# Hybrid decoder layer on one core: a weight chunk split ahead of the query/key rotations, and the last norm's 1/sqrt by ScalarE's estimate and one Newton step

## The chip, the cores and the metric

One core of one Trainium2 chip runs the whole layer in one launch. The metric is the device time of an execution in microseconds (us); three executions of the kernel before gave 813.43, 814.51 and 815.0 us, so its median is 814.51 us. The engines are called as the profile calls them: PE (TensorE matmul), PEld (its weight load), DVE (VectorE), ACT (ScalarE), POOL (GpSimd), SP (the queue that issues most DMAs).

## What is computed

One layer on 512 tokens of width 1024, all in float32. It has three sub-layers, each with a norm before and after: attention and retention in parallel, cross-attention to 256 memory rows, and a SwiGLU feed-forward.

```python
def rms_norm(x, g):
    y = x * lax.rsqrt(jnp.mean(x * x, axis=-1, keepdims=True) + 1e-6)
    return y * g

def hybrid_mixer(h, w_in, attn_gn_g, ret_gn_g, w_out):
    proj = h @ w_in                                  # 1024 -> 3*512 + 4*512
    aq, ak, av, rq, rk, rv, rg = jnp.split(proj, splits, axis=-1)
    a = dilated_attention(rope(aq), rope(ak), av)    # 8 heads x 64, then a norm per head
    r = retention(rope(rq), rope(rk) * 128 ** -0.5, rv)   # 4 heads x 128, then a group norm
    r = jax.nn.silu(rg) * r
    return jnp.concatenate([a, r], axis=-1) @ w_out

def reference(x, mem, ...):
    x = x + rms_norm(hybrid_mixer(rms_norm(x, pre_mix_g), ...), post_mix_g)
    x = x + rms_norm(memory_cross_attn(rms_norm(x, pre_mem_g), mem, ...), post_mem_g)
    x = x + rms_norm(swiglu(rms_norm(x, pre_ffn_g), w_gate_up, w_down), post_ffn_g)
    return x
```

## The kernel before, in words

**Split weights.** Each float32 operand of a projection is kept as a high part and a low part, and each product takes three matmuls: high by high, high by low, low by high (`mm3`, L84 to L86). A weight chunk of 128 x 2048 floats (1 MB) arrives by a DMA from SP into one of two `raw` buffers (L152). `split` then makes the high part `wh` on ACT (L90, two pieces of 128 x 1024) and the low part `wl` on DVE (L91, two pieces); `wl` needs `wh`. Each pair `wh`, `wl` takes two of the 20 buffers ("units") of one pool, which also holds the transposed input, the rotation tables, and the queries and keys. `take` hands a chunk over and splits further ones in advance; `ahead` splits up to a named chunk. Chunks of `w_in` are numbered as they are used: 0 to 3 retention's queries and keys, 4 and 5 its values, 6 and 7 its gate, 8 and up attention.

**The place of the first edit.** The first stage makes retention's queries and keys, in eight tiles f = 0 to 7 that fill all eight PSUM banks (`rqk`, `pss`). After the first half of the sum the kernel calls `ahead("w_in", 4)`, computes the input's row norm, and finishes the eight tiles one after the other. The norm factor is spread to all partitions by four small matmuls (`bcast_row`, L222) and multiplied into the rotation tables on POOL (L288). Then each tile is rotated: three DVE instructions (L291 to L293, into `t1` and `t2`) and an addition on POOL (L294). Tile 0 is first copied to `sc`, so its rotation reads SBUF alone; the others read PSUM. A bank is free again once its rotation has read it. Then `tok_proj(4, "rv", ...)` makes the values: four token blocks, each 24 matmuls, 12 with chunk 4 and 12 with chunk 5. After them come the gate's blocks (`rg`, chunks 6 and 7).

**What sets the order.** Outside of the feed-forward, which is written out by hand, a scheduler orders the instructions of each engine at build time, by the order of the code, the free buffers and its own costs. On the chip every engine works its list strictly in that order and waits on semaphores. So DVE's list decides when a low part is made, and a rotation that stands ahead of it must be done first. SP's list is ordered likewise: a `raw` buffer is filled again once both parts of the chunk in it are made.

**The place of the second edit.** The feed-forward's last product is made for four blocks of 128 rows, each in two halves of 512 columns (tile `dn`). `residual` (L664 to L676) closes a block: for each half ACT squares it with a row sum (L670), DVE multiplies it by the gain (L671, tile `z`) and adds the sum to `v` (L672, tile `pv`); then `rsqrt` (L180 to L184) makes 1/sqrt(v) on DVE from an integer guess and three Newton steps of two instructions; then `z` times this factor is added to `x` (L676), and two DMAs write the block out, one from SP's queue, one from ACT's (L1065). Nothing stands behind the last block, so its `residual` is the kernel's end.

Of the kernel before, what the change touches and what calls it, by code (L numbers as in the profile page):

```python
# [15 lines left out]
AF = mybir.ActivationFunctionType  # L16
ALU = mybir.AluOpType
AX = mybir.AxisListType

P = 128  # L20
D = 1024
# [3 lines left out]
TB = S // P  # L25
# [6 lines left out]
EPS = 1e-6  # L32
# [6 lines left out]
def hybrid_layer(ctx, tc, t, out):  # L39
    nc = tc.nc  # L40
# [9 lines left out]
    def uname(p):  # L50
        cnt[0] += 1
        return f"{p}{cnt[0]}"

    def bank(name):
        return psp.tile([P, 512], F32, tag="ps", name=uname(name))
# [10 lines left out]
    def row(name):  # L66
        return wk.tile([P, D], F32, tag="w4k", name=uname(name), bufs=2)

    def junk():
        return wk.tile([P, D], BF16, tag="junk", name=uname("junk"), bufs=1)  # L70

    def small(shape, name):
        big = math.prod(shape[1:]) > 8
        return sm.tile(shape, F32, tag="big" if big else "tiny", name=uname(name), bufs=2 if big else 32)
# [67 lines left out]
    def load(pieces=1, swap=False):  # L142
        key = chunks.pop(0)
        src = t[key[0]][key[1]]
        raw = fetched.pop(key, None)
        w = pair("w")
        if raw is None:
            raw = rawp.tile([P, 2048], F32, tag="raw", name=uname("raw"))
            n = 2048 // pieces
            for i in range(pieces):  # L150
                c = slice(i * n, (i + 1) * n)
                nc.sync.dma_start(raw[:, c], src[:, c])  # L152
        n = 2048 // max(2, pieces)
        for i in range(max(2, pieces)):
            c = slice(i * n, (i + 1) * n)
            if swap and i == 0:
                nc.vector.tensor_copy(w[0][:, c], raw[:, c])
                nc.vector.tensor_sub(w[1][:, c], raw[:, c], w[0][:, c].bitcast(F32))
            else:
                split(raw[:, c], w[0][:, c], w[1][:, c])  # L160
        loaded[key] = w

    def take(name, i, ahead=2):
        while (name, i) not in loaded:
            load()
        while chunks and len(loaded) - 1 < ahead:
            load()
        return loaded.pop((name, i))

    def ahead(name, i):  # L170
        while (name, i) in chunks:
            load()

    def rsqrt(v, n, name, e=None):
        e = e or nc.vector
        y = small([P, n], name + "y")
        w = small([P, n], name + "w")
        if n == 1:
            nv = small([P, 1], name + "n")
            e.tensor_scalar(y.bitcast(I32), v.bitcast(I32), -0.5, 1597463007.0, op0=ALU.mult, op1=ALU.add)  # L180
            e.tensor_scalar_mul(nv, v, -0.5)
            for _ in range(3):
                e.tensor_scalar(w, y, y, nv, op0=ALU.mult, op1=ALU.mult)
                e.tensor_scalar(y, w, 1.5, y, op0=ALU.add, op1=ALU.mult)  # L184
            return y
        nc.vector.tensor_scalar(y.bitcast(I32), v.bitcast(I32), -0.5, 1597463007.0, op0=ALU.mult, op1=ALU.add)
        for _ in range(3):
            nc.vector.tensor_mul(w, y, y)
            nc.vector.scalar_tensor_tensor(w, w, -0.5, v, op0=ALU.mult, op1=ALU.mult)
            nc.vector.scalar_tensor_tensor(y, w, 1.5, y, op0=ALU.add, op1=ALU.mult)  # L190
        return y

    def row_rstd(rows, n, width, name, eps=EPS, e=None):
        ss = small([P, n], name + "s")
        for i, r in enumerate(rows):
            nc.scalar.activation(junk()[:, :width], r, AF.Square, accum_out=ss[:, i:i + 1])
        v = small([P, n], name + "v")
        (e or nc.vector).tensor_scalar(v, ss, 1.0 / width, eps, op0=ALU.mult, op1=ALU.add)
        return rsqrt(v, n, name, e)
# [8 lines left out]
    def load_gains(*names):  # L208
        u = unit("g")
        out = []  # L210
        for i, name in enumerate(names):
            src = t[name]
            out.append(u[:, i * D:(i + 1) * D])
            nc.sync.dma_start(out[-1], bass.AP(tensor=src.tensor, offset=src.offset, ap=[[0, P], [1, D]]))
        return out
# [25 lines left out]
    ones = cp.tile([P, P], F32, name="ones")  # L241
# [13 lines left out]
    w_rqk = [take("w_in", i, 0) for i in range(4)]  # L255
# [8 lines left out]
    pss = [bank("rqk") for _ in range(8)]  # L264

    def rqk(f, k):
        w = w_rqk[k // 2]
        mm3(pss[f], part(w, (k % 2) * D + f * P, P), hx(k, 0, S), k == 0, k == KT - 1)

    for k in range(4):  # L270
        for f in range(8):
            rqk(f, k)
    ahead("w_in", 4)
    rstd0 = row_rstd(x, TB, D, "r0")
    rbc = None
    for f in range(8):
# [191 lines left out]
    scale = AD ** -0.5  # L468
# [190 lines left out]
    att_out(3)  # L659
    w_out = {c: take("w_out", c, 0) for c in (2, 3, 0, 1)}  # L660

    def residual(pss, b, g, e=None, cuts=((0, 512), (512, 512))):
        e = e or nc.vector
        ss = small([P, len(cuts)], "ps")  # L664
        z = row("z")
        v = small([P, 1], "pv")
        for i, (c0, n) in enumerate(cuts):
            c = slice(c0, c0 + n)
            ps = pss[c0 // 512][:, c0 % 512:c0 % 512 + n]
            nc.scalar.activation(junk()[:, :n], ps, AF.Square, accum_out=ss[:, i:i + 1])  # L670
            nc.vector.tensor_mul(z[:, c], ps, g[:, c])  # L671
            e.tensor_scalar(v, ss[:, i:i + 1], 1.0 / D, v if i else EPS, op0=ALU.mult, op1=ALU.add)  # L672
        rs = rsqrt(v, 1, "pr", e)
        for c0, n in cuts:
            c = slice(c0, c0 + n)
            nc.vector.scalar_tensor_tensor(x[b][:, c], z[:, c], rs, x[b][:, c], op0=ALU.mult, op1=ALU.add)  # L676
# [44 lines left out]
    def mix_half(hf, mid=None):  # L721
        bs = (2 * hf, 2 * hf + 1)
        pss = out_proj(bs, y_lhs, w_out, order, "o1", 2, mid)
        hs = []
        for b in bs:
            e = nc.gpsimd if b == 3 else nc.vector
            residual(pss[b], b, g1, e)
            hs.append(normed(b, g2, e))
        return hs
# [102 lines left out]
    def mem_block(b, mid=None):  # L832
        pss = out_proj((b,), o_lhs, wo, nat, "o2", 0, mid)[b]
        with tc.high_priority(600):
            residual(pss, b, g3, nc.vector)
            return normed(b, g4, nc.vector)
# [195 lines left out]
    pss = [[bank("dn") for _ in range(2)] for _ in range(TB)]  # L1032
# [3 lines left out]
    cuts = [halves] * TB  # L1036

    def down(b, c0, n, k, w):
        mm3(pss[b][c0 // 512][:, c0 % 512:c0 % 512 + n], part(aT[k // 4], (k % 4) * S + b * P, P),
            part(w, (k % 2) * D + c0, n), k == 0, k == FT - 1)  # L1040

    for c in range(FT // 2 - NL):
        if c % 2 == 0:
            split_a(c // 2 + 1)
        w = take("w_dn", c)
# [8 lines left out]
    g5, = load_gains("post_ffn_g")  # L1054
# [4 lines left out]
    for b in range(TB):  # L1059
        for c0, n in cuts[b]:  # L1060
            for k in range(FT - 2 * NL, FT):
                down(b, c0, n, k, ws[k // 2 - (FT // 2 - NL)])
        residual(pss[b], b, g5, cuts=cuts[b])
        for i, (c0, n) in enumerate(cuts[b]):
            (nc.sync, nc.scalar)[i % 2].dma_start(out[b * P:(b + 1) * P, c0:c0 + n], x[b][:, c0:c0 + n])  # L1065

# [95 lines left out]
```

## Time and profile before

| | |
|---|---|
| median of the three runs | 814.51 us (813.43 to 815.0) |
| the profiled execution's own time | 813.49 us |
| its span, first to last instruction | 811.7 us |
| busy: PE, DVE, ACT, POOL | 97%, 62%, 47%, 24% of the span |
| mean granted TensorE clock | 0.994 |

In a row of the timeline stand the start in us, the duration in us, engine, line, operation, output and input, and the count where equal rows were merged; in brackets stands the idle time of the engine before it and what ended this idle time. The chain of waits lists who waited for whom: total us, times, longest. Matmuls overlap: each takes 0.39 us in the rows, but at full clock one starts every 0.227 us.

### The profile page before, as it was taken

What the parts mean: (1) busy time and instruction counts of PE and PEld (TensorE: products, weight loads), DVE (VectorE), ACT (ScalarE), POOL (GpSimd) and SP (SyncE); (2) the same over time, 40 slices, a digit from 0 to 9 for tenths busy, and PEclk for the clock granted to TensorE, in tenths of its full rate; (3) what the DMA queues carried; (4) which work ended last, traced back from release to release, by engine and by line L of the source; (5) the groups of instructions that cost most, each with busy time, mean ns of one, the idle gap of its engine ahead of it and who ended that gap; (6) DMA issues with size and microseconds to landing.
All of it is one profiled execution on the core that took longest, in us unless ns stands there. A gap on an engine that the chain in (4) does not pass through costs nothing.

```text
span 811.7 us, 12194 instructions
## 1 busy us (share of the span) xinstructions
PE 790.5 (97%) x4828; PEld 696.5 (86%) x4828; DVE 503.5 (62%) x1007; ACT 384.4 (47%) x664; POOL 196.8 (24%) x169
## 2 busy tenths in 40 slices
PE   9989999999999999999999989999999999999995
PEld 8767888876777888999988989999999998888884
DVE  6496158865565646857656697667777766541144
ACT  6504343557555642535527386555555545432011
POOL 0161024330110110210000463333333326551000
PEclk9999999999999999999999999999999999999998
DMA  8616211231112650414205468777777783764011
GB/s 328 255 52 233 105 52 53 94 114 53 53 52 104 258 209 1 156 54 160 100 27 141 145 164 251 209 208 207 209 208 209 210 258 132 308 245 169 1 52 52
DMA packets 23849, 119.55 MB, mean 147 GB/s; under 512 B 2800, under 2 KB 2800, under 8 KB 14320
## 3 DMA queue, kind: packets, MB, share of 16 engines
q1 hardware_dynamic: 19904, 99.89, 33.3%
q0 software_dynamic: 3168, 17.83, 12.0%
q10 hardware_dynamic: 720, 1.06, 0.3%
q8 instruction: 38, 0.62, 0.3%
q14 instruction: 19, 0.16, 0.1%
HBM read 108.80 MB, written 9.96 MB: 146 GB/s over the span
## 4 chain that ended last, share of the span: by engine, by line
PE 76%; DVE 12%; issue 4%; POOL 3%; ACT 3%; DMA 1%; DVEq 0%; SPq 0%; ACTq 0%; POOLq 0%
PE dn L84 5%; PE dn L86 5%; PE dn L85 5%; PE p L84 3%; PE o L85 3%; PE p L86 3%; PE p L85 3%; PE o L84 3%; PE o L86 3%; PE q L85 3%; PE q L86 3%; PE q L84 3%; DVE wl L91 3%; PE r L84 2%; PE r L85 2%
## 5 line engine op out<-in xcount | busy, mean ns | idle before, releaser
L91 DVE TENSOR_TENSOR wl<-raw,wh 128x1024 fp32r<-128x1024 f32 (+1 forms) x91 | 118.0, 1330 | 66.1 <-ACT wh L90 39.6
L90 ACT CAST wh<-raw 128x1024 fp32r<-128x1024 f32 (+1 forms) x91 | 90.1, 1038 | 69.4 <-DMA raw<-in_w_in 37.9
L91 DVE TENSOR_TENSOR wbl<-sums,wbh 128x1024 fp32r<-128x1024 f32 x40 | 51.2, 1280 | 30.3 <-ACT wbh L90 30.3
L84 PE MATMUL dn<-wh,ah 128*128 128x512 f32 x176 | 68.5, 389 | 0.0
L85 PE MATMUL dn<-wl,ah 128*128 128x512 f32 x176 | 68.5, 389 | 0.0
L86 PE MATMUL dn<-wh,al 128*128 128x512 f32 x176 | 68.5, 389 | 0.0
L135 POOL DMA_DIRECT2D wal<-in_w_gu x22 | 19.6, 889 | 176.3 <-ACT wal L134 117.7
L1022 POOL TENSOR_TENSOR al<-af,ah 128x512 fp32r<-128x512 f32 x22 | 36.1, 1672 | 43.9 <-ACT ah L1021 43.9
L84 PE MATMUL p<-bB,wah 128*128 128x256 f32 x160 | 45.3, 283 | 0.0
L85 PE MATMUL p<-bB,wah 128*128 128x256 f32 x160 | 45.3, 283 | 0.0
L86 PE MATMUL p<-bB,wal 128*128 128x256 f32 x160 | 45.3, 283 | 0.0
L90 ACT CAST wbh<-sums 128x1024 fp32r<-128x1024 f32 x40 | 40.2, 1051 | 3.3 <-POOL sums L125 1.8
L125 POOL TENSOR_TENSOR sums<-raw,sums 128x512 f32<-128x512 f32 x20 | 34.1, 1704 | 25.4 <-DVE sums L125 25.4
L86 PEld LDWEIGHTS dn<-wh,al 128*128 128x128 f32 x176 | 33.0, 188 | 6.9
L85 PEld LDWEIGHTS dn<-wl,ah 128*128 128x128 f32 x176 | 33.0, 188 | 6.8
L84 PEld LDWEIGHTS dn<-wh,ah 128*128 128x128 f32 x176 | 33.0, 188 | 6.8
L134 ACT ACTIVATE wal<-wah 128x768 fp32r<-128x768 f32 (+1 forms) x48 | 36.6, 810 | 0.0
L85 PE MATMUL q<-hhl,wh 128*128 128x256 f32 x128 | 36.2, 284 | 0.2 <-DVE hhl L91 0.2
L84 PE MATMUL q<-hhh,wh 128*128 128x256 f32 x128 | 35.8, 284 | 0.3 <-ACT hhh L90 0.3
L86 PE MATMUL q<-hhh,wl 128*128 128x256 f32 x128 | 36.1, 283 | 0.0
L131 ACT CAST wah<-raw 128x768 fp32r<-128x768 f32 (+1 forms) x48 | 35.9, 804 | 0.0
L915 ACT ACTIVATE c<-c 128x512 f32<-128x512 f32 x20 | 12.6, 632 | 49.1 <-DVE c L914 49.1
(337 smaller groups left out, 2522.2 us busy)
## 6 DMA issues: line engine op xcount, KB each, us to landing
raw<-in_w_gu SPq DMA_DIRECT2D x22, 1024.0 KB, 5.0
wal<-in_w_gu POOLq DMA_DIRECT2D x20, 768.0 KB, 7.5
raw<-in_w_in SPq DMA_DIRECT2D x12, 1024.0 KB, 4.9
raw<-in_w_dn SPq DMA_DIRECT2D x11, 1024.0 KB, 4.8
raw<-in_w_kv SPq DMA_DIRECT2D x8, 1024.0 KB, 4.7
ad<-c SPq DMA_DIRECT2D x20, 256.0 KB, 4.1
af<-ad SPq DMA_DIRECT2D x5, 1024.0 KB, 7.0
x<-in_x SPq DMA_DIRECT2D x4, 1024.0 KB, 9.7
```

What stands on the lines that cost most here:

```text
L84: nc.tensor.matmul(o, lhsT=sh, rhs=mh, start=start, stop=False)
L85: nc.tensor.matmul(o, lhsT=sh, rhs=ml, start=False, stop=False)
L86: nc.tensor.matmul(o, lhsT=sl, rhs=mh, start=False, stop=stop)
L90: nc.scalar.copy(hi, src)
L91: nc.vector.tensor_sub(lo, src, hi.bitcast(F32))
L125: e.tensor_sub(*{"s2": (s2, s1, a11), "s3": (s3, a11, a21), "s4": (s4, a12, s2)}[name])
L131: nc.scalar.copy(w[0][:, c], raws[f][:, c])
L134: nc.scalar.mul(w[1][:, c], w[0][:, c].bitcast(F32), -1.0)
L135: nc.gpsimd.dma_start(w[1][:, :n], t["w_gu"][f][:, :n], accum_op=ALU.add)
L915: nc.scalar.activation(c, c, AF.Silu)
L1022: nc.gpsimd.tensor_sub(lo[:, c], v[:, c], hi[:, c].bitcast(F32))
```

## The change

It has two parts that do not touch each other.

```diff
@@ the first stage
     for k in range(4):
         for f in range(8):
             rqk(f, k)
-    ahead("w_in", 4)
+    w_rqk[0] = w_rqk[1] = None
+    ahead("w_in", 5)
     rstd0 = row_rstd(x, TB, D, "r0")
@@ residual, and the function that it now calls
+    def root(ss, v0, v):
+
+        y, w = small([P, 1], "ey"), small([P, 1], "ew")
+        nc.scalar.activation(y, ss, AF.Abs_reciprocal_sqrt, bias=v0, scale=1.0 / D)
+        nv = small([P, 1], "en")
+        nc.vector.tensor_scalar_mul(nv, v, -0.5)
+        nc.vector.tensor_scalar(w, y, y, nv, op0=ALU.mult, op1=ALU.mult)
+        nc.vector.tensor_scalar(y, w, 1.5, y, op0=ALU.add, op1=ALU.mult)
+        return y
+
-    def residual(pss, b, g, e=None, cuts=((0, 512), (512, 512))):
+    def residual(pss, b, g, e=None, cuts=((0, 512), (512, 512)), last=False):
         e = e or nc.vector
         ss = small([P, len(cuts)], "ps")
         z = row("z")
         v = small([P, 1], "pv")
+        if last:
+            nc.scalar.activation(junk()[:, :1], ones[:, :1], AF.Abs_reciprocal_sqrt)
         for i, (c0, n) in enumerate(cuts):
             c = slice(c0, c0 + n)
             ps = pss[c0 // 512][:, c0 % 512:c0 % 512 + n]
             nc.scalar.activation(junk()[:, :n], ps, AF.Square, accum_out=ss[:, i:i + 1])
+            if last and i:
+                v0, v = v, small([P, 1], "pv")
+                e.tensor_scalar(v, ss[:, i:i + 1], 1.0 / D, v0, op0=ALU.mult, op1=ALU.add)
+                rs = root(ss[:, i:i + 1], v0, v)
             nc.vector.tensor_mul(z[:, c], ps, g[:, c])
-            e.tensor_scalar(v, ss[:, i:i + 1], 1.0 / D, v if i else EPS, op0=ALU.mult, op1=ALU.add)
-        rs = rsqrt(v, 1, "pr", e)
+            if not (last and i):
+                e.tensor_scalar(v, ss[:, i:i + 1], 1.0 / D, v if i else EPS, op0=ALU.mult, op1=ALU.add)
+        if not last:
+            rs = rsqrt(v, 1, "pr", e)
@@ the last loop
-        residual(pss[b], b, g5, cuts=cuts[b])
+        residual(pss[b], b, g5, cuts=cuts[b], last=b == TB - 1)
```

Chunk 5 is split before the row norm and the rotations instead of when the values begin; for its room, chunks 0 and 1 (of the queries and keys, whose half of the sum is done) are dropped there. In the last block, ACT makes an estimate of 1/sqrt straight from the second half's row sum, with the first half's `v` as bias, and DVE makes one Newton step of it. A small activation of the same function stands ahead of the block, so that ACT's table for it is loaded there.

Line numbers below are those of each kernel: behind the first edit the changed kernel's are one higher, so the rotation's L291 to L294 are L292 to L295 there.

DVE's list in the first stage, kernel before: `wl_284` is chunk 4's low part, `wl_482` chunk 5's, `wl_490` and `wl_498` are those of chunks 6 and 7; `t_347` and `t_348` are tile 0's rotation, `t_365` and `t_366` tile 1's, `t_473` and `t_474` tile 7's.

```order
L91 TENSOR_TENSOR wl_284<-raw_285,wh_283 128x1024 x2
L291 TENSOR_TENSOR t_347<-sc_326,rope_164 128x512
L292 TENSOR_TENSOR t_348<-sc_326,rope_164 64x512
L293 TENSOR_TENSOR t_348<-sc_326,rope_164 64x512
L291 TENSOR_TENSOR t_365<-rqk_180,rope_164 128x512
```

Tiles 1 to 7 follow in the same manner, and behind the last of them, still before:

```order
L291 TENSOR_TENSOR t_473<-rqk_186,rope_164 128x512
L292 TENSOR_TENSOR t_474<-rqk_186,rope_164 64x512
L293 TENSOR_TENSOR t_474<-rqk_186,rope_164 64x512
L91 TENSOR_TENSOR wl_482<-raw_483,wh_481 128x1024 x2
L91 TENSOR_TENSOR wl_490<-raw_491,wh_489 128x1024 x2
L91 TENSOR_TENSOR wl_498<-raw_499,wh_497 128x1024 x2
```

So chunk 5's low part waits there for 24 rotation instructions. DVE's first place in the changed kernel, where chunk 5's low part is called `wl_292` (behind tile 7 there, `wl_490` follows at once):

```order
L91 TENSOR_TENSOR wl_284<-raw_285,wh_283 128x1024 x2
L292 TENSOR_TENSOR t_355<-sc_334,rope_164 128x512
L293 TENSOR_TENSOR t_356<-sc_334,rope_164 64x512
L91 TENSOR_TENSOR wl_292<-raw_293,wh_291 128x1024 x2
L294 TENSOR_TENSOR t_356<-sc_334,rope_164 64x512
L292 TENSOR_TENSOR t_373<-rqk_180,rope_164 128x512
```

Chunk 5's two DVE pieces have moved from behind all eight rotations into the middle of the first; nothing else on DVE moves there, and the list of ACT is the same in both (its casts of chunk 5 stood ahead of the rotations already).

SP's list at the same place, before and then after (`rtab` is a table for retention, `raw_499` chunk 7, `raw_617` chunk 8):

```order
L152 DMA raw_491<-in_w_in 128x2048
L152 DMA raw_499<-in_w_in 128x2048
L152 DMA raw_617<-in_w_in 128x2048
L325 DMA rtab_609<-in_rtab 128x1024
L152 DMA raw_625<-in_w_in 128x2048
```

```order
L152 DMA raw_491<-in_w_in 128x2048
L152 DMA raw_499<-in_w_in 128x2048
L326 DMA rtab_609<-in_rtab 128x1024
L152 DMA raw_617<-in_w_in 128x2048
L152 DMA raw_625<-in_w_in 128x2048
```

The table's load now stands ahead of chunk 8's. On PE only the first two blocks of the values differ: before, block 1 (`rv_531`) begins after the first matmul with chunk 5, in the middle of block 0 (`rv_505`); in the changed kernel block 0 is finished first.

DVE's list at the end, last block, before and then after:

```order
L671 TENSOR_TENSOR z_7657<-dn_6911,g_7360 128x512
L672 TENSOR_SCALAR pv_7658<-ps_7656,pv_7658 128x1
L180 TENSOR_SCALAR pry_7667<-pv_7658 128x1
L181 TENSOR_SCALAR prn_7669<-pv_7658 128x1
L183 TENSOR_SCALAR prw_7668<-pry_7667,prn_7669 128x1
L184 TENSOR_SCALAR pry_7667<-prw_7668,pry_7667 128x1
L183 TENSOR_SCALAR prw_7668<-pry_7667,prn_7669 128x1
L184 TENSOR_SCALAR pry_7667<-prw_7668,pry_7667 128x1
L183 TENSOR_SCALAR prw_7668<-pry_7667,prn_7669 128x1
L184 TENSOR_SCALAR pry_7667<-prw_7668,pry_7667 128x1
L676 SCALAR_TENSOR_TENSOR x_7357<-z_7657,pry_7667,x_7357 128x512 x2
```

```order
L686 TENSOR_SCALAR pv_7667<-ps_7656,pv_7658 128x1
L688 TENSOR_TENSOR z_7657<-dn_6911,g_7360 128x512
L668 TENSOR_SCALAR en_7672<-pv_7667 128x1
L669 TENSOR_SCALAR ew_7670<-ey_7669,en_7672 128x1
L670 TENSOR_SCALAR ey_7669<-ew_7670,ey_7669 128x1
L695 SCALAR_TENSOR_TENSOR x_7357<-z_7657,ey_7669,x_7357 128x512 x2
```

Five small instructions fewer stand in the list, and `pv` now comes ahead of the multiplication into `z`. ACT's list at the end of the changed kernel, from the last square of block 2 (`dn_6909`) on:

```order
L683 ACTIVATE junk_7589,ps_7582<-dn_6909 128x512
L679 ACT_TABLE_LOAD
L679 ACTIVATE junk_7659<-ones 128x1
L1084 DMA out<-x_7357 128x512
L683 ACTIVATE junk_7661,ps_7656<-dn_6910 128x512
L683 ACTIVATE junk_7665,ps_7656<-dn_6911 128x512
L666 ACTIVATE ey_7669<-ps_7656,pv_7658 128x1
L1084 DMA out<-x_7357 128x512
```

The table load and the small activation have come in ahead of block 2's output DMA, and the estimate (`ey`) behind the last square; no second table load stands between the square and the estimate.

## The prediction

> **What bounds the kernel now.** I read the page's first part, then the chain of waits of PE, then the timeline of the two places that the change touches.
>
> ```profile
> span 811.7 us, 12194 instructions
> PE 790.5 (97%) x4828; PEld 696.5 (86%) x4828; DVE 503.5 (62%) x1007; ACT 384.4 (47%) x664; POOL 196.8 (24%) x169
> PE rv L85 <- DVE wl L91: 5.1, 1, 5.1
> PE p L84 <- DVE c L910: 3.8, 2, 2.1
> ```
>
> PE is busy for 97% of the span: whatever does not shorten PE's own work can only gain where PE waits, or at the end, where nothing is left for it. The third row is the longest wait that PE has in the whole execution, and it happens once: the value product (`rv`, its matmul with a low weight part) waits 5.1 us for that part from DVE. The next, in the feed-forward, is not touched. This is the timeline around the longest wait:
>
> ```profile
> 34.91 2.00 ACT L90 CAST wh<-raw 128x1024 fp32r<-128x1024 f32 x2 [0.42 <-DMA raw<-in_w_in]
> 37.35 3.45 DVE L91 TENSOR_TENSOR wl<-raw,wh 128x1024 fp32r<-128x1024 f32 x2
> 37.51 7.82 POOL L288 TENSOR_TENSOR rope<-rope,rbc 128x512 f32<-128x512 f32 x4 [36.08 <-DVE rbc L223]
> 44.20 1.68 DVE L293 TENSOR_TENSOR t<-sc,rope 64x512 f32<-64x512 f32 x1
> 45.91 0.69 DVE L291 TENSOR_TENSOR t<-rqk,rope 128x512 f32<-128x512 f32 x1
> 47.32 0.68 DVE L293 TENSOR_TENSOR t<-rqk,rope 64x512 f32<-64x512 f32 x1
> 51.55 0.39 PE L84 MATMUL rv<-wh,hTh 128*128 128x512 f32 x1
> 56.54 0.39 PE L84 MATMUL rv<-wh,hTh 128*128 128x512 f32 x1
> 60.07 0.68 DVE L293 TENSOR_TENSOR t<-rqk,rope 64x512 f32<-64x512 f32 x1
> 60.79 5.71 DVE L91 TENSOR_TENSOR wl<-raw,wh 128x1024 fp32r<-128x1024 f32 x4
> 62.07 0.80 PE L85 MATMUL rv<-wl,hTh 128*128 128x512 f32 x1 [5.14 <-DVE wl L91]
> 65.40 0.40 PE L84 MATMUL rv<-wh,hTh 128*128 128x512 f32 x1
> 69.07 2.00 ACT L90 CAST wh<-raw 128x1024 fp32r<-128x1024 f32 x2 [21.48 <-DMA raw<-in_w_in]
> 70.16 2.36 DVE L91 TENSOR_TENSOR wl<-raw,wh 128x1024 fp32r<-128x1024 f32 x2 [3.65 <-ACT wh L90]
> 80.17 0.39 PE L84 MATMUL rg<-wh,hTh 128*128 128x512 f32 x1
> 62.07:65.40 3.33, 3.33 (x9) 2.67 (x9) 3.33 (x3) 0.00 (x0) 1.08 (x1) 0.55 0.13 17
> 65.40:70.00 4.60, 4.60 (x22) 3.78 (x21) 1.10 (x1) 0.93 (x1) 0.00 (x0) 1.00 0.93 378
> ```
>
> ACT has cast chunk 5's high part by 36.91 us, but DVE makes its low part only at 60.79, when the last rotation (60.07) is through. PE has begun the values at 51.55, comes to the low part after 56.54 and goes on at 62.07. The last two rows are stretches of time, with the busy time of PE, PEld, DVE, ACT and POOL and the granted clock: for 3.33 us behind the wait PE runs at 0.55 of its clock, from 65.40 on at 1.00. So the stop costs more than the wait. The Trainium skill, "TensorE: Matmul & The Clock Gate", section "What's actually happening", says that the clock falls to half after an idle window of about 3.4 us and comes back after as long a busy one; the two stretches agree. By that rule a wait shorter than a window would cost its length alone.
>
> **The change, first part.** *What the stop costs.* Between 51.55 and 56.54 stand 22 steps from matmul to matmul, so one step is 4.99 / 22 = 0.2268 us. The matmul at 65.40 is the ninth behind that at 56.54 (the stretch counts nine matmuls from 62.07 on, the last of them cut). Without a stop it would begin at 56.54 + 9 x 0.2268 = 58.58. The stop costs 65.40 - 58.58 = 6.82 us, of which 5.14 are the wait and 1.68 the slow matmuls.
>
> *When the low part comes now.* Its two DVE pieces stand behind the second instruction of tile 0's rotation, so they begin at 44.20, where L293 began. Two such pieces take 2.36 us alone (70.16) and 3.45 beside POOL's multiplications (37.35). POOL is done at 37.51 + 7.82 = 45.33, so of the first 1.13 us each piece goes at 3.45 / 2 = 1.73, which does 0.65 of one; the other 1.35 take 1.18 each, 1.59 in all. The low part is ready at 46.9, between 46.6 and 47.7. PE gets to it at 51.55 + 13 x 0.2268 = 54.50. The wait is gone with 6.8 us to spare.
>
> *What is late instead.* The rotations. Tile 0's third instruction took 1.68 us beside POOL; alone I take the 0.68 of tile 1's (47.32), and keep 1.68 as its other end. Then tile 1 begins at 47.6 instead of 45.91, 1.7 us later (1.3 to 3.5). Value block 1 needs tile 1's bank: PE comes there at 51.55 + 24 x 0.2268 = 56.99, and the rotation is over at 48.00 + 1.7 = 49.7, 51.5 at the latest. Each further block takes PE 5.44 us and each rotation about 2.13 (eight of them from 40.7 to 60.75), so PE never catches up. The last rotation ends at 62.4 (64.3 at the latest) and chunk 6's low part at 62.4 + 2.4 = 64.8, at most 64.3 + 3.45 = 67.7; PE needs it when the gate begins, at 80.17 - 6.82 = 73.35. Chunk 7's raw buffer comes free when the low part of chunk 5 is made, some 17 us sooner than now. But even if it came no sooner than now, its low part would be ready at 70.16 + 2.36 = 72.5, and PE wants it twelve matmuls into the gate, at 76.1. On SP's queue the table is moved ahead of chunk 8: it waits for PE's use of a query/key chunk, which is over at 51.55, and chunk 8's buffer is not free before chunk 6's low part at 64.8, so it is held up by nothing. ACT's list is the same; it was idle for 21.48 us before 69.07. POOL's additions shift with the rotations, and their first reader on PE comes behind two gate blocks, after 73.35 + 2 x 5.44 = 84.2. Dropping chunks 0 and 1 issues nothing. The first part is worth 6.82 us, as long as PE stays unbroken from there; from 70 us on each engine waits for PE or for weights that PE's progress lets in, so I take the shift to carry to the end.
>
> **The change, second part.** Two views, the timeline of the end and the groups of instructions of ACT:
>
> ```profile
> 793.04 0.19 ACT L670 ACTIVATION_READ_ACCUMULATOR junk<-dn 128x1 f32 x1
> 797.49 0.34 ACTq L1065 DMA_DIRECT2D out<-x  x1
> 803.43 0.60 ACT L670 ACTIVATE junk<-dn 128x512 bf16<-128x512 f32 x1 [4.75 <-PE dn L86]
> 803.92 0.19 ACT L670 ACTIVATION_READ_ACCUMULATOR junk<-dn 128x1 f32 x1
> 804.15 0.69 DVE L671 TENSOR_TENSOR z<-dn,g 128x512 f32<-128x512 f32 x1 [4.69 <-ACT junk L670]
> 804.76 0.20 DVE L672 TENSOR_SCALAR pv<-ps,pv 128x1 f32<-128x1 f32 x1
> 805.00 0.15 DVE L180 TENSOR_SCALAR pry<-pv 128x1 int32<-128x1 int32 x1
> 805.07 0.14 DVE L181 TENSOR_SCALAR prn<-pv 128x1 f32<-128x1 f32 x1
> 805.25 0.27 DVE L183 TENSOR_SCALAR prw<-pry,prn 128x1 f32<-128x1 f32 x1
> 805.55 0.21 DVE L184 TENSOR_SCALAR pry<-prw,pry 128x1 f32<-128x1 f32 x1
> 806.67 0.21 DVE L184 TENSOR_SCALAR pry<-prw,pry 128x1 f32<-128x1 f32 x1
> 806.92 1.42 DVE L676 SCALAR_TENSOR_TENSOR x<-z,pry,x 128x512 f32<-128x512 f32 x2
> 808.37 0.34 ACTq L1065 DMA_DIRECT2D out<-x  x1
> L244 ACT ACT_TABLE_LOAD x1 | 1.3, 1283 | 1.2 <-PEq L1151 1.2
> L244 ACT ACTIVATE junk<-ones 128x1 bf16<-128x1 f32 x1 | 0.3, 297 | 0.0
> ```
>
> After the last row sum (804.11) only DVE works: 806.92 - 804.15 = 2.77 us from `z` to the addition into `x`. In the new list `pv` goes first, at 804.15; `z` needs nothing of it and begins 0.07 later (as from 805.00 to 805.07), or 0.24 if it has to wait as a reader does (804.76 to 805.00). Then, from start to start: `z` 0.61 (804.15 to 804.76), `en` 0.18 (805.07 to 805.25), `ew` 0.30 (805.25 to 805.55), `ey` 0.25 (806.67 to 806.92). The sum is 1.41 to 1.58 us against 2.77; I take the longer, a gain of 1.19 us (at most 1.36). The estimate on ACT is no row of before; the nearest is the 128x1 activation of 0.297 us. From 804.15 it ends at 804.45, and DVE wants it at 804.15 + 0.24 + 0.61 + 0.18 = 805.18, so 0.7 us cover it. The table load (1.283) and the small activation (0.297) come behind block 2's last row sum, at 793.23, and are over by 794.8, ahead of the DMA at 797.49 and of all that ACT does for block 3: no cost.
>
> **The sum.** 6.82 + 1.19 = 8.01 us off the profiled execution's 813.49 gives 805.5. The median of the runs stands 1.02 us above that execution, so I forecast 814.51 - 8.01 = 806.5 us.
>
> **Rivals.** *The table is loaded once more.* If squares and the estimate were in different tables, a load would stand between the last square and the estimate: 804.11 + 1.28 + 0.30 = 805.7, 0.5 us after DVE wants it, so 0.7 of the 1.19 stay and the time is 807.0. Against it: the new list holds one load, ahead of both. The Trainium skill, "ScalarE: Activation LUTs", section "What ACT_TABLE_LOAD costs", counts a drain with each switch, about 2.66 us in all; by that figure the estimate would be late by 1.9 us and the tail 0.7 us slower than before, 808.4 us.
>
> *The wait moves to the gate.* DVE splits no less than before, and PE reaches the gate 6.8 us sooner. For a wait of 2 us there, chunk 7's low part would have to come at 78.1, 5.6 us later than even in the old order; that gives 808.5, and 1.7 more if the clock falls again. For it speaks only that DVE's pieces stretch beside POOL (3.45 against 2.36).
>
> *The split does not get away from the rotations.* If the freed buffers did not reach chunk 5, PE would wait as before and only the tail would gain: 813.3, which is no change. The list of DVE speaks against it.
>
> *Slower.* All eight rotations, and with them the banks, now stand behind chunk 5's cast and its transfer. If that came late, value block 1 would wait for tile 1's bank. It decides when the rotations slip by more than 8.0 us beyond the 7.3 that lie between 49.7 and 56.99: the cast would have to end at about 59 us instead of 36.91. At 2 us beyond that the time is 816.5.
>
> **Chances.** The forecast 84%, the second table load 5%, the wait at the gate 5%, the split still behind the rotations 3%, slower 3%. A measurement of this kernel tells about 0.2% (1.6 us) from no change. The first three are faster (0.94), the fourth is the same (0.03), the last slower (0.03). The forecast's own bounds are 814.51 - 8.18 and, with a late `z` and rotations, little over 806.5; the runs before lie 1.1 us below and 0.5 above their median. So the range runs from 804.8, a low run with the larger tail gain, to 808.6, which takes in the second table load and a short wait at the gate.
>
> **What the profile after would show.** The chain of waits of PE has no row of `rv` waiting for `wl`; two pieces of L91 stand near 44 to 47 us between rotations; no stretch of half clock near 62; the gate begins near 73.4; the addition into `x` begins 1.2 us sooner after the last row sum; ACT's table load lies near 786.5. I am wrong if PE shows a new wait of over 1 us between 54 and 110, or if the end does not move with the gate's start.

## The result, and the profile after

The changed kernel took 805.45 us (median; 805.34 to 807.16 in 4 runs), the kernel before beside it 814.75 (813.43 to 818.10 in 4). The ratio is 0.9885, with a 95% interval of 0.9852 to 0.9917: faster by 1.15%. The forecast was 806.5, between 804.8 and 808.6. The profiled execution is the slowest of the four: 807.16 us, its span 805.4, against 813.49 and 811.7 before.

The page's first part after the change, and the chain of waits of PE (in all, times, longest):

```profile
span 805.4 us, 12197 instructions
PE 790.4 (98%) x4828; PEld 696.7 (87%) x4828; DVE 503.4 (62%) x1002; ACT 386.4 (48%) x667; POOL 197.7 (25%) x169
PE p L84 <- DVE c L929: 3.9, 2, 2.1
PE warm L261 <- POOL ones L242: 1.0, 1, 1.0
```

The row of `rv` waiting for `wl` is gone; the feed-forward's waits, second before, are now the longest. PE's work is the same to 0.1 us. So what the span lost is time in which PE stood or ran slowly, and a part of the end. The timeline of the first place (start, us, engine line):

```profile
42.46 1.66 DVE L293 TENSOR_TENSOR t<-sc,rope 64x512 f32<-64x512 f32 x1
44.15 3.35 DVE L91 TENSOR_TENSOR wl<-raw,wh 128x1024 fp32r<-128x1024 f32 x2
47.52 0.69 DVE L294 TENSOR_TENSOR t<-sc,rope 64x512 f32<-64x512 f32 x1
48.24 0.69 DVE L292 TENSOR_TENSOR t<-rqk,rope 128x512 f32<-128x512 f32 x1
62.41 0.68 DVE L294 TENSOR_TENSOR t<-rqk,rope 64x512 f32<-64x512 f32 x1
63.12 5.73 DVE L91 TENSOR_TENSOR wl<-raw,wh 128x1024 fp32r<-128x1024 f32 x4
73.22 0.39 PE L84 MATMUL rg<-wh,hTh 128*128 128x512 f32 x1
```

Chunk 5's two pieces (44.15) stand inside tile 0's rotation, and its last instruction behind them. The last rotation ends at 63.09, the gate begins at 73.22. In stretches of time (length, then busy time of PE, PEld, DVE, ACT, POOL, and the granted clock), the values run without a break, and there is no half clock behind 62:

```profile
51.55:56.77 5.22, 5.22 (x25) 4.32 (x24) 5.06 (x9) 2.01 (x2) 2.85 (x3) 1.00 0.28 116
56.77:62.07 5.30, 5.30 (x25) 4.40 (x24) 5.17 (x8) 0.69 (x1) 3.60 (x3) 1.00 0.00 0
62.07:65.40 3.33, 3.33 (x16) 2.75 (x16) 3.29 (x4) 0.69 (x1) 2.50 (x2) 1.00 0.00 0
478.07:481.48 3.41, 1.38 (x12) 1.41 (x12) 3.41 (x3) 2.90 (x4) 2.70 (x2) 1.00 1.04 281
481.48:484.90 3.42, 3.06 (x15) 2.76 (x14) 2.14 (x5) 1.09 (x2) 2.04 (x2) 0.50 1.00 419
```

The last two rows lie elsewhere, behind a feed-forward wait that both kernels have: there the clock falls to half for 3.42 us in this execution. It did not in the profiled execution of before. This is the timeline of the end:

```profile
788.16 1.28 ACT L679 ACT_TABLE_LOAD   x1
798.83 0.19 ACT L683 ACTIVATION_READ_ACCUMULATOR junk<-dn 128x1 f32 x1
799.06 0.29 ACT L666 ACTIVATE ey<-ps,pv 128x1 f32<-128x1 f32 x1
799.06 0.21 DVE L686 TENSOR_SCALAR pv<-ps,pv 128x1 f32<-128x1 f32 x1 [4.69 <-ACT junk L683]
799.19 0.68 DVE L688 TENSOR_TENSOR z<-dn,g 128x512 f32<-128x512 f32 x1
799.79 0.14 DVE L668 TENSOR_SCALAR en<-pv 128x1 f32<-128x1 f32 x1
800.04 0.27 DVE L669 TENSOR_SCALAR ew<-ey,en 128x1 f32<-128x1 f32 x1
800.35 0.21 DVE L670 TENSOR_SCALAR ey<-ew,ey 128x1 f32<-128x1 f32 x1
800.59 1.42 DVE L695 SCALAR_TENSOR_TENSOR x<-z,ey,x 128x512 f32<-128x512 f32 x2
```

From the last row sum's read to the addition into `x` it is 800.59 - 798.83 = 1.76 us. Before, it was 806.92 - 803.92 = 3.00.

Where the time came from: from the values' first matmul to the gate's, 80.17 - 51.55 = 28.62 us have become 73.22 - 51.46 = 21.76, a gain of 6.86; the end gives 1.24; together 8.10. Of the profiled pair's difference (813.49 - 807.16 = 6.33) the half clock at 481.48 took back 1.2, and 0.6 went near 291, where a cast waited for a chunk's DMA. The other three runs, which left no trace, stand at 805.3 to 805.5, 8.0 to 8.2 below 813.49; a later execution of the changed kernel that was traced (`e8` below, 805.60) has neither of the two losses.

### The profile page after: what moved, and what is told of

Its sections match the earlier page's. It is cut to its first block, busy times and chain, and to the rows that moved or that the text cites. A ratio compares the mean times of both kernels' runs of the same rounds, so it can differ in the third digit from the quotient of the medians.

```text
span 805.4 us, 12197 instructions
## 1 busy us (share of the span) xinstructions
PE 790.4 (98%) x4828; PEld 696.7 (87%) x4828; DVE 503.4 (62%) x1002; ACT 386.4 (48%) x667; POOL 197.7 (25%) x169
## 4 chain that ended last, share of the span: by engine, by line
PE 77%; DVE 10%; ACT 5%; POOL 3%; issue 3%; DMA 1%; DVEq 0%; POOLq 0%; ACTq 0%
PE dn L85 5%; PE dn L84 5%; PE dn L86 5%; PE p L84 3%; PE p L86 3%; PE p L85 3%; DVE wl L91 3%; PE q L85 3%; PE q L86 3%; PE q L84 3%; PE o L85 3%; PE o L86 3%; PE o L84 3%; PE r L84 2%; PE r L85 2%
## 5 line engine op out<-in xcount | busy, mean ns | idle before, releaser
L91 DVE TENSOR_TENSOR wl<-raw,wh 128x1024 fp32r<-128x1024 f32 (+1 forms) x91 | 120.6, 1359 | 64.7 <-ACT wh L90 38.4
```

Source lines behind the costliest of these rows:

```text
L91: nc.vector.tensor_sub(lo, src, hi.bitcast(F32))
```

## The experiments

Where an expectation speaks of a theory by letter or number, the name holds for that expectation alone.

**Both parts again, and each alone.** `e1_both` is the changed kernel; its ratio and those of the next three come from the same chip, with 20 runs of the kernel before (median 814.59).

> The changed kernel once more, in more executions. Theory: the change is worth the stop of the value product (5.1 us of waiting and 1.7 us of half clock, 6.9 us by the start of the gate in the two traces) and 1.2 us at the end; what else differs between executions is one window of 3.4 us at half clock where the feed-forward begins, 1.2 to 1.8 us, which comes or stays away with the phase of the clock gate. So executions lie near 805.4 us at a mean clock of 0.997, or near 807.1 us at 0.996, and before lies near 813.5 or 815.0. Rival: the 1.8 us that were lost at 290 and 482 us in the profiled execution come from the change itself (work that now comes sooner collides there), then most executions lie near 807.

It took 807.45 us (805.30 to 808.56), ratio 0.9910 (0.9896 to 0.9924). One of the five executions lies near 805.4; the others, at 806.34 to 808.56, are not all near 807.1. The profiled one lost its time in a place that the expectation does not name, by a fall of the clock at 176.81. The rival, that the losses at 290 and 482 come from the change itself, does not hold: in the traces of `e1` and `e8` PE runs through both places without them.

The first part alone is the kernel before with

```diff
-    ahead("w_in", 4)
+    w_rqk[0] = w_rqk[1] = None
+    ahead("w_in", 5)
```

> The first part alone: chunk 5 split ahead, the old 1/sqrt at the end. Theory: 6.9 us faster than before in executions of the same clock, so near 806.6 us, with no wait of rv for wl and the gate near 73.2 us. Rival (the stop's clock part comes back elsewhere): 5.2 us faster, near 808.3.

It took 808.37 us (806.96 to 810.85), ratio 0.9929 (0.9915 to 0.9943). From the first value matmul to the gate it takes 21.76 us, as in the changed kernel; the tail stays at 804.27 - 801.27 = 3.00. The median is at the rival's 808.3 and the lowest run near the theory's 806.6. In the first stage nothing is given back. Both figures were set off the profiled execution of before (813.49), a low one; from the median beside it the gain is 6.2 us, between the two.

The second part alone is the changed kernel with the old split:

```diff
-    w_rqk[0] = w_rqk[1] = None
-    ahead("w_in", 5)
+    ahead("w_in", 4)
```

> The second part alone: the old place of the split, the estimate and one Newton step at the end. Theory: 1.2 us faster than before, near 812.2 us; from the last row sum to the addition into x 1.76 us instead of 3.00; the value product still waits 5.1 us and then runs 3.4 us at half clock. Rival (the tail is hidden or paid by the table load): no change, 813.5.

It took 813.14 us (812.57 to 815.69), ratio 0.9986 (0.9977 to 0.9995). Its chain of waits has the old row back, with the half clock behind it, and its tail is the new one (804.49, 806.25: 1.76 us, as forecast); only the half clock is longer than expected, 6.82 us instead of 3.4:

```profile
PE rv L85 <- DVE wl L91: 5.2, 1, 5.2
...
58.66:65.48 6.82, 3.97 (x9) 3.14 (x10) 6.76 (x7) 0.00 (x0) 3.07 (x2) 0.50 0.12 19
...
804.49 0.19 ACT L682 ACTIVATION_READ_ACCUMULATOR junk<-dn 128x1 f32 x1
806.25 1.42 DVE L694 SCALAR_TENSOR_TENSOR x<-z,ey,x 128x512 f32<-128x512 f32 x2
```

The medians give 6.2 us for the first part, 1.45 for the second, 7.65 in sum, and 7.1 for both at once, within the spread of the runs: the parts add. Over all runs of the study the median is 814.83 for the kernel before (43 runs) and 806.37 for the changed one (19): 8.5 us, where the single sets give 9.3, 7.1, 9.0 and 7.0. The line that gives up the two query/key chunks did none of it: built without that line, the five engines' lists and waits are the same, row for row. (That version was not run.)

**How much the place of the split is worth, and when the clock falls.** The changed kernel with the split moved behind tile 4's or tile 5's rotation:

```diff
     w_rqk[0] = w_rqk[1] = None
-    ahead("w_in", 5)
+    ahead("w_in", 4)
...     (in the loop over the tiles, at its end)
+        if f == 4:        # 5 in the other kernel
+            ahead("w_in", 5)
```

> The changed kernel, but chunk 5 is split behind the rotation of tile 4 instead of in tile 0. The low part's first piece is then ready at about 55.7 us and PE comes for it at 54.7, so PE waits about 1 us. Theory (the clock falls when PE is idle for most of a window of 3.4 us): full clock, cost 1 us of PE's place, the gate near 74.2. Rival (any stop lowers the clock): 3.4 us of half clock behind it, the gate near 75.9.

> The same with the split behind tile 5: the first piece is ready at about 57.8, PE waits about 3.1 us, a little under the 3.4 us of a window. Theory A (a window has to be idle as a whole): full clock, the gate near 76.3. Theory B (idle for about half of a window is enough, as in the feed-forward's first step): half clock for 3.4 us behind the wait if the wait falls into one window for the larger part, the gate near 78.0.

One execution each: 806.98 us (span 805.2) behind tile 4, 811.09 (809.3) behind tile 5. These are PE's waits with the split behind tile 4 (two waits) and behind tile 5 (one), and for the latter the stretch before the fall and the stretch at half clock:

```profile
PE rv L85 <- DVE wl L91: 1.6, 2, 1.0
```

```profile
PE rv L85 <- DVE wl L91: 3.2, 1, 3.2
...
54.75:58.16 3.41, 0.51 (x2) 0.47 (x3) 3.35 (x5) 0.00 (x0) 2.55 (x2) 1.00 0.00 0
58.16:61.57 3.41, 3.41 (x9) 2.43 (x9) 3.38 (x4) 0.00 (x0) 0.57 (x1) 0.50 0.21 41
```

From the first value matmul to the gate: 23.97 and 26.87 us, where the early split has 21.76 and the old order 28.62. So two waits of 1.6 us in sum cost 2.2, and one of 3.16 costs 5.1, because the clock falls behind it. With tile 4 the gate begins at 75.06, between the two forecasts (74.2 and 75.9), but at full clock, as the theory has it: there were two waits, where one had been expected. With tile 5 it begins at 78.26 with half clock behind the wait: theory B. So the gain goes with the stop that PE still has, and the price jumps where the stop becomes long enough for the clock.

**The table load.** The changed kernel without the small activation ahead of the last block:

```diff
-        if last:
-            nc.scalar.activation(junk()[:, :1], ones[:, :1], AF.Abs_reciprocal_sqrt)
```

> The changed kernel without the small activation ahead of the last block, so that the table load stands between the last square and the estimate. By the rows of before (load 1.28 us, small activation 0.30): the estimate ends 1.28 us later, at 1.6 us behind the last row sum, where DVE wants it after 1.0, so the end comes about 0.6 us later than in the changed kernel. Rival, by the Trainium skill's figure for a switch with its drain, an estimate of 2.66 us: 1.9 us later.

One execution: 805.96 us. The load now stands between the last square and the estimate:

```profile
797.01 0.19 ACT L681 ACTIVATION_READ_ACCUMULATOR junk<-dn 128x1 f32 x1
797.22 1.28 ACT L666 ACT_TABLE_LOAD   x1
798.51 0.29 ACT L666 ACTIVATE ey<-ps,pv 128x1 f32<-128x1 f32 x1
798.84 0.27 DVE L669 TENSOR_SCALAR ew<-ey,en 128x1 f32<-128x1 f32 x1 [0.74 <-ACT ey L666]
799.40 1.41 DVE L693 SCALAR_TENSOR_TENSOR x<-z,ey,x 128x512 f32<-128x512 f32 x2
```

The tail is 799.40 - 797.01 = 2.39 us: 0.63 longer than with the early load, as forecast (0.6), and still 0.61 shorter than before. So half of the second part's gain hangs on that one activation. The load lasts its own 1.28 and nothing is added to it: it begins 0.02 us behind the read of the row sum. "ScalarE: Activation LUTs" of the Trainium skill, section "What ACT_TABLE_LOAD costs", counts a drain with each switch, some 2.66 us in all; at this place no drain is seen.

**A look at the wait that is left.** In the feed-forward's first step PE waits 2.15 us for the addition `c` (L929) and then 0.36 for `s` (L975; 0.48 in `e8`, at full clock). In the last step it waits for `c` once more: 1.71 us in the profiled execution, but 2.20, 2.36 and 3.30 in those of `e1`, `e8` and `e11`, the same program. These are the two waits together in `e11`, with the longest last:

```profile
PE p L84 <- DVE c L929: 5.5, 2, 3.3
```

The first try moved these additions and the step's preparation:

```diff
     (in the first step only)
+        c11 and s1+r ahead of the split of block pair 1
-        blocks_sum(f + 2, ...), blocks_b(f + 1, 0), blocks_a(f + 2) at their old places
+        the same three behind the addition u, at the step's end
```

> The changed kernel, and in the first written-out step of the feed-forward DVE makes the additions that PE waits for ahead of the two splits and sums for later steps. Theory: the waits of 2.15 and 0.36 us there go, and with them the window of half clock that hangs on them, so 2.5 us faster than the changed kernel at full clock, near 802.9 us, and no execution with a lower mean clock. Rival (DVE has more work than the step leaves room for): the wait moves to the next step, which needs the splits, and the time stays near 805.4.

It took 810.77 us (809.81 to 814.46), ratio 0.9960 (0.9945 to 0.9974): 3.3 us slower than the changed kernel beside it. Neither the theory nor the rival foresaw that. The first step's wait for `c` is gone, and PE stands longer for a transfer:

```profile
PE p L86 <- DMA wal<-in_w_gu: 6.1, 1, 6.1
```

POOL sent that weight block at 476.22 instead of 474.19, and it took 9.6 us or more to land where the changed kernel's took 6.9 to 7.9. A low-part transfer that had been hidden became the bound.

The second try leaves the preparation where it is and puts only `c11` first, in every step:

```diff
+        ffn_c11(f)
         if nxt:
             blocks_b(f + 1, 1)
         else:
             load()
-        ffn_c11(f)
```

> The changed kernel once more, beside the next run. All theories: 805.3 to 807.5 us, a ratio to the kernel before of 0.990. If the fall of the clock after a stop of 2 to 3 us is a matter of where PE's idle time lies in the clock's window (theory B), some executions show granted 0.998 (no fall), some 0.995 or 0.996 (one fall, 1.6 to 1.9 us more), and the same program may show both. If a fall belonged to the program (theory A), all executions of one program show the same place.

> The changed kernel, and in every feed-forward step the addition c11 stands ahead of DVE's splits of that step instead of behind them; transfers and splits keep their places. In the changed kernel's trace c11 stands behind 3.5 us of DVE work at 475.5 to 479.5 in the first step and behind 4.16 us of splits at 670.80 in the last; PE waits there 2.15, 0.48 and 1.88 us. Theory 1 (the waits are DVE's order alone, and only the moved transfers spoiled the earlier reordering): the waits at 480.1 and 673 go; PE then wants the weights sent at 474.19, which land 6.9 to 7.9 us later at 481.1 to 482.1, about 1 us sooner than now, so 0 to 1 us is given back; 801.5 to 803 us where the changed kernel has 805.4, and no half-clock window behind 480. Theory 2 (these weights' transfer is what bounds the first step, as in the earlier reordering): a wait for wal of 2 us or more takes the place of the first wait, only the last step's 1.9 us are gained, or less: 803.5 to 806 us.

The changed kernel took 806.13 us (805.60 to 807.67), ratio 0.9891 (0.9872 to 0.9910), as expected; its profiled execution has no fall, and the one profiled first has one, so the falls do not belong to the program (theory B). `c11` first took 806.30 (805.72 to 806.78), ratio 0.9888 (0.9869 to 0.9908): the same. Neither of its theories foresaw it: the first wait moved one instruction on.

```profile
PE r L84 <- DVE s L975: 3.1, 2, 2.8
...
476.54 0.41 DVE L929 TENSOR_TENSOR c<-s,p 128x256 f32<-128x256 f32 x1
476.87 4.19 DVE L91 TENSOR_TENSOR wbl<-sums,wbh 128x1024 fp32r<-128x1024 f32 x2
480.99 0.41 DVE L975 TENSOR_TENSOR s<-s,r 128x256 f32<-128x256 f32 x1
```

`c` is done by 476.95, but both splits now stand ahead of `s`, and PE wants `s` before it goes on with `r`. The last step's wait did shrink, from 2.36 to 0.38. But behind the wait for `s` the clock fell for 6.82 us in this execution, which took 2.6 us (against PE's starts in `e8`), about as much as the last step gave.

The third try moves `c11` in the first and last step only, and in the first `s1+r` ahead of the second split as well:

```diff
+        if f in (PRE, FT - 1):
+            ffn_c11(f)
...     (its old place keeps it for the other steps)
+        if f == PRE:
+            nc.vector.tensor_add(s1[:, H:], s1[:, :H], r[:, :H])
         if nxt:
             blocks_b(f + 1, 0)
```

> The changed kernel, and in the first feed-forward step c11 stands ahead of DVE's split for block pair 1, and the addition s1+r ahead of the split for pair 0; in the last step c11 stands ahead of the two splits of load. The other steps are as they were. With c11 alone moved, s1+r stood behind 4.19 us of splits (476.87 to 480.99) and PE waited 2.75 us for it. Theory 1 (the waits are DVE's order alone): PE reaches r 2.9 us behind c11's end and finds DVE free, so of 2.15 + 0.48 us in the first step at most 0.5 stay; the last step's wait falls from 1.9 to 2.4 to about 0.4. Gain 3.5 to 4.5 us on the changed kernel's executions without a fall (span 803.8): a span near 800, 801.5 to 803 us, and no half-clock window behind 480. Theory 2 (the weights' transfer sent at 473.4 bounds the first step): PE waits for wal from 480.2 up to their landing, 480.5 to 481.5, so 0.3 to 1.3 of it is given back; 802.5 to 804.

> The changed kernel beside the run before it: 805.3 to 807.5 us. Executions with granted clock 0.997 to 0.999 stand near 805.5, those with 0.995 or 0.996 some 1 to 1.9 us higher, by one half-clock window of 3.41 us each, not always at one place.

It took 803.51 us (802.62 to 806.01 in 4 runs), ratio to the kernel before 0.9859 (0.9834 to 0.9884); the changed kernel beside it 807.80 (805.33 to 808.65 in 6), ratio 0.9898 (0.9875 to 0.9920). Three of the four runs (802.62, 802.85, 804.18) lie below all 19 of the changed kernel in this study, and the median is 4.3 us lower; the two intervals overlap a little. So this version is faster than the kernel before by 1.4%, and than the changed kernel by some 0.5% in this one comparison of four runs with six. The median lies where theory 2 put it, but the trace shows theory 1's mechanism in the first step: no wait for `wal`, and 0.55 us left of the waits there. The profiled execution is the one at 806.01. There the gain of the first step is seen, and a loss in the next:

```profile
PE p L84 <- DVE c L929: 3.0, 1, 3.0
...
479.03 0.41 DVE L975 TENSOR_TENSOR s<-s,r 128x256 f32<-128x256 f32 x1
485.72 0.69 DVE L123 TENSOR_TENSOR sums<-raw 128x512 f32<-128x512 f32 x1 [2.67 <-DMA raw<-in_w_gu]
```

The weights that SP sent from 474 to 489 us took 7.6 to 9.8 us to land there, 5.0 to 5.1 in the profiled execution of the changed kernel and 5.2 to 5.5 in that of the second try; so DVE's sums, and with them `c` of the second step, came late. Whether this is that execution's transfer alone stays open: the other three runs are 1.8 to 3.4 us faster, and have no trace.

**When the clock falls: one table out of all traces.** The records of the clock change only on a grid of 3.41 us, whose place against the program differs from execution to execution. The table takes stretches of that grid that ran at full clock and held little work for PE, in order of PE's busy time in the view of stretches: all behind which the clock fell (but one, told below), and some of the next above them, behind which it did not (eight more stand between 1.66 and 1.78). The first stretch and those of the end of the span are left out:

```
kernel                      stretch          PE busy   clock in the next stretch
before                      58.27:61.68      0.00      0.50
earlier reordering (e4)     481.15:484.57    0.00      0.50
split behind tile 5 (e6)    54.75:58.16      0.51      0.50
first alone (e2)            673.93:677.34    0.95      0.50
changed, again (e11)        672.65:676.06    0.97      0.50
second alone (e3)           55.24:58.66      1.11      0.50
changed (profiled)          478.07:481.48    1.38      0.50
c11 first (e9)              477.28:480.70    1.41      0.50
earlier reordering (e4)     675.71:679.12    1.58      0.50
split behind tile 5 (e6)    481.41:484.82    1.59      1.00
split behind tile 4 (e5)    477.45:480.86    1.65      1.00
changed, again (e8)         477.66:481.07    1.66      1.00
before                      484.94:488.35    1.67      1.00
changed (profiled)          672.63:676.04    1.70      1.00
split behind tile 4 (e5)    54.20:57.61      1.80      1.00
```

The bound lies near 1.6, and the rows at 1.58 and 1.59 can't be told apart: with its stretch moved by 0.01 us the second is 1.58 too. A stretch with 1.57 at the end of `e8` (795.11 to 798.52) brought no fall either.

The same stop of 2.15 us at 480 thus costs only itself in `e8`, and 1.2 us more in the profiled execution. There nearly the whole stop lies in one stretch (it ends at 480.10, the stretch runs from 478.07 to 481.48). In `e8` the stop ends at 479.05, and its first part lies ahead of the stretch that begins at 477.66:

```profile
477.66:481.07 3.41, 1.66 (x12) 1.49 (x12) 3.41 (x4) 3.41 (x5) 2.06 (x1) 1.00 1.01 311
481.07:484.48 3.41, 3.29 (x27) 3.29 (x28) 3.06 (x6) 1.08 (x2) 2.21 (x2) 1.00 1.04 401
```

One fall does not fit: in `e1` at 176.81, behind a stretch in which the view has PE busy for 3.08 us, but with ten matmuls only, most of them shorter or of 64 rows. Busy time is modelled there, and the table can't say how such matmuls count.

## Why the prediction was right, by its own steps

*What the stop costs: right.* 6.82 us forecast, 6.86 measured, and 21.76 us from the first value matmul to the gate in each of the nine profiled executions with the early split. The split into 5.14 of wait and 1.68 of slow matmuls is borne out in kind by tile 5's run, where 3.16 of wait cost 5.1; but not all of the rest is clock: in tile 4's run, at full clock, two waits of 1.61 in sum cost 2.2, some 0.3 more for each. The Trainium skill, "TensorE: Matmul & The Clock Gate", section "What's actually happening", gives half clock after at least one idle window of about 3.4 us. The prediction took from it that a wait shorter than a window costs its length alone. That does not hold here: 3.16 us, less than the 3.41, brought the fall, and so did 2.15. The same section of the Trainium skill says that the windows run freely; the table agrees, and adds that a window need not be idle.

*When the low part comes: a size off.* Ready at 47.50, forecast 46.9 (46.6 to 47.7). The two pieces took 3.35 us, not 2.72. A narrower stretch of the timeline after shows the first one alone:

```profile
44.15 2.21 DVE L91 TENSOR_TENSOR wl<-raw,wh 128x1024 fp32r<-128x1024 f32 x1
```

So it took 2.21 us, and the second, from 46.28 on, 1.21. I had halved the 3.45 of a pair at 37.35, as if there were a slower pace beside POOL. But that pair was uneven too (1.22, and 2.31 from 38.48 on), and its first piece ran beside POOL at full pace. The two slow pieces are those that began while a POOL multiplication was under way, and each ended 1.1 us behind it (POOL 39.71, piece 40.79; POOL 45.27, piece 46.36), about the length of a piece alone. They look as if they had waited for it, so what counts is when POOL's multiplication ends; no run tried that. PE needed the part 7 us later, so it changed nothing.

*What is late instead: right, a size off.* Tile 1 began at 48.24, 2.3 us later than before, forecast 1.7 (1.3 to 3.5), by the longer split. The last rotation ended at 63.09 (62.4 forecast, 64.3 at the latest). Neither the banks nor the gate waited: the two rivals that put a wait there have no row in the chain of waits of any execution with the early split. SP's exchange of the table with chunk 8, POOL's additions and ACT's casts held up nothing on PE.

*The second part: right.* 1.24 us for 1.19. `pv` to `z` took 0.13 us (799.06 to 799.19), between the 0.07 and the 0.24 of the forecast. The estimate, costed by a 0.297 us activation of the same shape, took 0.29 and ran beside `pv` and `z`. The rival with a second load has its own run now: 0.5 forecast, 0.63 measured.

*The sum: 8.01 forecast, 8.10 by these two stretches.* The median came out 1.05 us below the forecast. The step concerned is the last, from the profiled execution to the median of the runs, for which I added 1.02 us because the median of before stood that much above its profile. In this set the surplus was not there: three of the four runs stand within 0.2 us of each other, at a mean granted clock of 0.997. In later sets the median was 807.45, 806.13 and 807.80, and over all 19 runs it is 806.37, close to the 806.5. So the term was sound, and the set on which the forecast was tested ran low; that the forecast would be met so closely over all runs is in part luck, since the term came from three runs. What makes the surplus is known in part: a fall of the clock cost 1.2 to 1.6 us in each of the three traced executions of the changed kernel that have one, and the wait for `c` in the last step differs by up to 1.6 (1.71 to 3.30). Most of the runs have no trace.

*The shift did not carry to the end.* I said that from 70 us on it would. In the profiled execution it did not quite: 6.95 us at the gate, 6.3 behind 291, 5.1 behind 485. The last step goes with the half clock, which the trace of `e8` lacks together with the loss; the one at 291, where the trace has a transfer that landed about 0.9 us later, was not tried.

## What to carry to other kernels

Where one engine is busy for 97% of the span, look for the row in its chain of waits that is long and happens once, and ask which instruction ahead of the releaser in the list can be done later; price the stop from the step before it to the step at which the pace is normal again, not by the wait alone. In the feed-forward such a move paid only where every addition that PE waits for came ahead of the splits and no transfer moved back: of three reorderings one was slower (a transfer went out 2 us later), one the same (an addition was left behind the splits), and the one that moved both additions and no transfer gained.

## What the runs showed that I had not expected

For stops of about 2 to 3.6 us the clock is a matter of chance. In the table, stretches with PE busy for up to 1.41 of 3.41 us bring half clock, from 1.65 on they don't, and of the two near 1.6 one does. As an estimate from that, with 1.6 / 3.41 = 0.47 as the bound: a single stop in otherwise full work brings no fall below 0.53 x 3.41 = 1.8 us, and always one above twice that, 3.6 us; between them the grid decides (the case of `e1` stands against the first half). By that, the old wait of 5.14 us paid it in every run; it did in the two that were profiled.

A fall lasts 3.41 us or 6.82: behind the old stop one stretch in the kernel before, two in the run of the second part alone. After a stretch at half clock with PE busy for 0.56, 2.15 or 2.66 us (`e3` from 58.66, `e4` from 484.57, `e9` from 480.70) a second one followed; after 3.03 or more (the kernel before from 61.68, and all others) the clock was full again. At half the pace, 2.66 to 3.03 us are the work of 1.3 to 1.5 us at full clock (an estimate), not far from the bound for the fall.

One execution of the first part alone ran with a granted clock of 0.95 nearly throughout (mean 0.944), neither half nor full:

```profile
300.00:420.00 120.00, 119.58 (x830) 111.61 (x829) 80.08 (x194) 53.40 (x124) 8.33 (x19) 0.95 0.23 84
```

In that stretch PE did 830 matmuls; the changed kernel did 831 in the same stretch at 1.00, and 830 in `e8`. So a granted clock of 0.95 cost these matmuls next to nothing here. Yet this execution is the slowest of its six, and between 146 and 264 us PE lost 0.8 us against `e8` in small steps, where the profiled changed kernel lost 0.04. Whether that hangs on the 0.95, and where it comes from, the runs don't show.
